# The second key's one-hot rows on ScalarE in three of four steps of the second gate half

## The chip, the core and the metric

The kernel runs on one NeuronCore of a Trainium2 chip. The time is device time in microseconds of one execution. TensorE multiplies matrices, VectorE and ScalarE work elementwise, GpSimd (POOL) issues the gathers, SyncE (SP) the large loads. A program decides on which engine each instruction stands and in which order; an engine takes its instructions in that order, and a semaphore holds it where data or a buffer is not ready.

## What is computed

Two layers of a hybrid backbone are applied to 128 context tokens and to 256 latent tokens. The part that matters here is PEER, a retrieval of single-neuron experts, at the end of each layer:

```python
s1 = einsum('thd,nd->thn', q[:, :, 0], k1)      # 8 heads, 128 first keys
s2 = einsum('thd,nd->thn', q[:, :, 1], k2)      # 128 second keys
v1, i1 = top_k(s1, 16);  v2, i2 = top_k(s2, 16)
...
top, pos = top_k(cand, 16)                      # 16 of the 256 sums per head
idx = i1 * 128 + i2 at pos;  g = softmax(top)
a = gelu(u_tab[idx] . x)
y = sum over head, k of g * a * v_tab[idx]
```

Each token chooses 8 x 16 = 128 of 16384 experts, and expert (i1, i2) has row 128 * i1 + i2 of the tables u and v.

## The kernel before

The 128 context tokens gather their rows from the tables (POOL, one gather of 128 rows at a time; VectorE multiplies them at L692 and L703). The 256 latent tokens do without a gather: all 16384 experts are computed densely, and a matrix of gates, zero for all but the chosen ones, masks the result. For block i of 128 experts (all second keys of first key i):

- **a_step** (L852) multiplies the u rows by the tokens and puts gelu of the result into the tile AR, two blocks at a time. In most of them the rows are split into a rounded part (uhi, by ScalarE, L846) and a rest (ulo, by VectorE, L847), so that three fast passes replace a slow one.
- **w_step** (from L857) makes the gates of 8 tokens for the 64 first keys of a half and multiplies them into AR. VectorE makes the one-hot rows m1 of the first key (L878) and e1 = m1 x gate (L883); e2 holds the one-hot rows of the second key, 8 tokens x 128 keys. Every second step VectorE makes e2 with one comparison (L876); in the others ScalarE makes it as relu(1 - |key - i2|), with one Abs for each token (L872) and one Relu over the tile (L874). TensorE multiplies e2 by e1, 16 matmuls of 64 columns (L890), into the PSUM tile psW, and VectorE multiplies psW into AR in two pieces (L897, the AR update).
- **o_step** (L926) multiplies two blocks of AR by the v rows and sums over all blocks in acc. In some of them AR is split into pp (L906 on ScalarE, L907 on VectorE) and v into vhi (L915) and vlo (L916).

AR holds 96 of the 128 blocks, so the work goes in two halves: the first 32 a_steps; the first gate half, 32 w_steps with 8 a_steps between; o_steps and a_steps in turn; the second gate half (hf = 1), 32 w_steps with 16 o_steps to go between; and the last 32 o_steps. This is done once in each layer. In layer 0 the second half also holds a modulation (matmuls psm) for layer 1.

```python
EA = 0.5
def frac(i, f):
    return int((i + 1) * f) > int(i * f)
```

`frac(n, EA)` says whether ScalarE makes the e2 of step n. e2, m1 and e1 come from a pool X with two buffers each, psW from a PSUM pool with two; so the e2 of a step can be written only when the matmuls of the step two before are done.

The order in which instructions stand on each engine isn't the order of the code: a scheduler reckons with durations of its own, and issues whichever piece of work it holds ready. It also decides where the o_step matmuls stand between the w_steps, and how the context's part and the latents' part of layer 1 interleave. A change of one instruction's engine can move rows everywhere behind it. In layer 1 the routing of the context ends in the tile ids (L676), the gathers need it, and each gather is multiplied on VectorE at L692; the latents' attention ends in out_proj (psol on TensorE, L524 and L525 on VectorE), a normalisation (L127 to L216), and m2xh (L147), from which the tokens for PEER are made.

Of the kernel before, what the change touches and what calls it, by code (L numbers as in the profile page):

```python
# [45 lines left out]
def tile_fn(ctx: ExitStack, tc, A, outs):  # L46
# [22 lines left out]
    def pS(tag, name):  # L69
        return banks[tag].tile([128, 512], F32, name=name, tag=tag)  # L70
# [679 lines left out]
    for l in range(DEPTH):  # L750
# [45 lines left out]
        with ExitStack() as es_:  # L796
# [15 lines left out]
            def AR(s, n):  # L812
                return ar[0][:, s:s + n, :] if s < 48 else ar[1 + (s >= 64)][:, (s - 48 if s < 64 else s - 64):(s - 48 if s < 64 else s - 64) + n, :]

            def seg_end(s):
                return 48 if s < 48 else 64 if s < 64 else NS
# [40 lines left out]
            def w_step(hf, n):  # L857
                t0 = n * TC
                rb = rt[t0 // 128]
                ts_ = slice(t0 % 128, t0 % 128 + TC)  # L860
                G = TC // TI
                e2 = X.tile([128, G, 128, TI], F16, name="e2", tag="e2")
                m1 = X.tile([128, G, HALF, TI], F16, name="m1", tag="m1")
                e1 = X.tile([128, G, 2, HALF, TI], F16, name="e1", tag="e1")

                def of_tokens(q):
                    return rb[:, q, ts_].rearrange("p (g t) -> p g t", t=TI)[:, :, None, :]

                if frac(n, EA):
                    nb_ = nid[t0 // 128]  # L870
                    for t in range(TC):
                        S.activation(e2[:, t // TI, :, t % TI], iota1, AF.Abs,  # L872
                                     bias=nb_[:, t0 % 128 + t:t0 % 128 + t + 1])
                    S.activation(e2, e2, AF.Relu, bias=1.0, scale=-1.0)  # L874
                else:
                    V.tensor_tensor(e2, iota16[:, None].to_broadcast([128, G, 128, TI]),  # L876
                                    of_tokens(1).to_broadcast([128, G, 128, TI]), op=OP.is_equal)
                mk_ = V.tensor_tensor(m1, iota16[:, None, hf * HALF:(hf + 1) * HALF].to_broadcast([128, G, HALF, TI]),  # L878
                                      of_tokens(0).to_broadcast([128, G, HALF, TI]), op=OP.is_equal)
                marks["W" if hf == 0 else "X"].append(mk_)  # L880
                g0 = t0 % 128 // TI
                gates = rg[t0 // 128][:, g0:g0 + G, :, None, :]
                V.tensor_tensor(e1, m1[:, :, None].to_broadcast([128, G, 2, HALF, TI]),  # L883
                                gates.to_broadcast([128, G, 2, HALF, TI]), op=OP.mult)
                pw = pS("t", "psW")
                pwv = pw.rearrange("p (t i) -> p t i", t=TC)
                for t in range(TC):
                    g, u = t // TI, t % TI
                    for q in range(2):
                        T.matmul(pwv[:, t, :], lhsT=e2[:, g, :, u], rhs=e1[:, g, q, :, u], start=(q == 0),  # L890
                                 stop=(q == 1))
                i = 0
                while i < HALF:
                    s0 = (hf * HALF + i) % NS
                    n_ = min(HALF - i, seg_end(s0) - s0)
                    av = AR(s0, n_)[:, :, t0:t0 + TC]
                    V.scalar_tensor_tensor(av, pwv[:, :, i:i + n_].rearrange("p t i -> p i t"), 1.0 / WSC, av, op0=OP.mult, op1=OP.mult)  # L897
                    i += n_
# [55 lines left out]
            for n in range(NW):  # L954
                w_step(0, n)
                if (n + 1) * PRE // NW > n * PRE // NW:
                    a_step(NA + n * PRE // NW)
# [3 lines left out]
            for n in range(NW):  # L961
                w_step(1, n)
                if (n + 1) * PRE // NW > n * PRE // NW:
                    o_step(NA - PRE + n * PRE // NW)
                if n % 8 == 7 and mods:
                    modulation(*mods.pop(0), "A")
# [30 lines left out]
            for k, r in RATES[l].items():  # L997
                ms = marks[k]
                n = int(len(ms) * r + 0.5)
# [14 lines left out]
EA = 0.5  # L1014
# [14 lines left out]
KA = 0.375  # L1029
KO = 0  # L1030
KO1 = 0


def frac(i, f):
    return int((i + 1) * f) > int(i * f)
# [6 lines left out]
def VSPLIT(l, ii):  # L1042
    return not frac(ii, KQ if NA - PRE <= ii < NA else KO if ii < 32 else KO1)

# [78 lines left out]
```

## Time and profile before

| | us |
|---|---|
| median of 3 runs (2414.77 to 2418.68) | 2416.36 |
| the profiled execution | 2407.9 |
| its span | 2406.1 |
| TensorE busy | 2260.6 |
| VectorE busy | 1904.6 |
| ScalarE busy | 1115.2 |
| second gate half, layer 0 | about 917 to 1045 |
| second gate half, layer 1 | about 2090 to 2214 |

The profiled execution is one of its own, 8.5 us shorter than the median of the runs; sums made from its rows are set against 2407.9. Busy time counts an engine's running instructions; matmuls overlap, so that TensorE counts as busy as long as they follow each other without a gap. The granted clock is the share of full speed at which TensorE was allowed to run in a stretch.

### The profile page before, as it was taken

Reading aid. Unit: us, or ns where it says so; the run is one execution under the profiler, and the core shown is the slowest. Engines: PE = TensorE matmul, PEld = TensorE weight load, DVE = VectorE, ACT = ScalarE, POOL = GpSimd, SP = SyncE. Lnnn points to the kernel's source line nnn. Section 1 sums busy time; section 2 is a strip of 40 time slices with the busy share of each in tenths; the row PEclk is TensorE's granted clock in tenths of the full one; section 3 lists DMA queues with packets and bytes.
Section 4 is the critical chain, followed back from the end, with each engine's and each line's share of the span. In section 5 each row is a group of like instructions: output and inputs, shape, how many; then the busy total and the mean of one; then the engine's idle time right before and its main releaser. Section 6 shows DMA issues by size and latency. Waiting matters only on the chain.

```text
span 2406.1 us, 41658 instructions
## 1 busy us (share of the span) xinstructions
PE 2260.6 (94%) x15660; PEld 1914.5 (80%) x15660; DVE 1904.6 (79%) x3942; ACT 1115.2 (46%) x2084; POOL 697.7 (29%) x523
## 2 busy tenths in 40 slices
PE   6999889999999999999989996989999999998997
PEld 5686469999998995667778785889999889855886
DVE  3157579996898888898863468899879888899987
ACT  3324532442785445444445553134348744444444
POOL 0000233454004433464200003435530143344630
PEclk8999989999999999999999998999999999998998
DMA  9967889999658999999863355989985599987994
GB/s 331 322 193 265 336 322 348 324 358 350 219 159 295 360 332 347 328 352 374 299 213 113 120 158 196 325 313 349 363 320 159 188 374 346 333 309 270 395 364 147
DMA packets 196314, 696.05 MB, mean 289 GB/s; under 512 B 22992, under 2 KB 27408, under 8 KB 196112
## 3 DMA queue, kind: packets, MB, share of 16 engines
q1 hardware_dynamic: 110016, 398.52, 46.7%
q0 software_dynamic: 74736, 272.14, 31.1%
q10 hardware_dynamic: 11360, 22.73, 2.8%
q8 instruction: 123, 2.02, 0.3%
q14 instruction: 79, 0.65, 0.1%
HBM read 689.14 MB, written 4.16 MB: 288 GB/s over the span
## 4 chain that ended last, share of the span: by engine, by line
PE 32%; DVE 8%; issue 8%; DMA 2%; POOL 1%; ACT 1%; DVEq 0%; ACTq 0%; POOLq 0%
PE acc L926 18%; PE psA L852 6%; DVE gt L692 2%; PE psil L262 2%; DMA gt<-in_peer_u_dram,ids 1%; POOL gt L686 1%; PE psqp L561 1%; PE psic L262 1%; DVE ulo L847 1%; PE psoc L522 1%; PE pssl L421 1%; DMA wic<-in_w_in_dram 1%; PE psW L890 0%; DVE idx L550 0%; DVE rep L548 0%
## 5 line engine op out<-in xcount | busy, mean ns | idle before, releaser
L686 POOL DMA_INDIRECT gt<-in_peer_u_dram,ids x256 | 325.3, 1271 | 1185.6 <-DVE gt L692 478.4
L686 POOL DMA_INDIRECT gt<-in_peer_v_dram,ids x256 | 368.0, 1438 | 464.0 <-DVE acc L703 434.7
L926 PE MATMUL acc<-vhi,pp 128*128 128x512 f32 x1728 | 441.9, 398 | 15.6 <-ACT pp L906 9.4
L852 PE MATMUL psA<-h2hi,uhi 128*128 128x256 f32 x1664 | 416.2, 287 | 5.1 <-ACT uhi L846 5.1
L852 PE MATMUL psA<-h2lo,uhi 128*128 128x256 f32 x1664 | 411.3, 284 | 0.0
L926 PEld LDWEIGHTS acc<-vhi,pp 128*128 128x128 f32 x1728 | 326.1, 191 | 86.3 <-ACT pp L906 10.0
L915 ACT ACTIVATE vhi<-v 128x1024 fp32r<-128x1024 f32 x216 | 228.7, 1060 | 274.0 <-PE acc L926 161.2
L692 DVE SCALAR_TENSOR_TENSOR gt<-gt,h2c 128x1024 f32<-128x1024 f32 x256 | 309.5, 1216 | 28.0 <-DMA gt<-in_peer_u_dram,ids 27.9
L703 DVE SCALAR_TENSOR_TENSOR acc<-gt,wcol,acc 128x1024 f32<-128x1024 f32 x254 | 325.5, 1282 | 6.2 <-DMA gt<-in_peer_v_dram,ids 5.2
L846 ACT ACTIVATE uhi<-u 128x1024 fp32r<-128x1024 f32 x208 | 220.0, 1058 | 230.2 <-PE psA L852 107.5
L852 PEld LDWEIGHTS psA<-h2hi,uhi 128*128 128x128 f32 x1664 | 319.7, 192 | 7.9 <-ACT uhi L846 5.7
L852 PEld LDWEIGHTS psA<-h2lo,uhi 128*128 128x128 f32 x1664 | 320.0, 192 | 2.1
L847 DVE TENSOR_TENSOR ulo<-u,uhi 128x1024 fp32r<-128x1024 f32 x208 | 254.3, 1223 | 79.9 <-ACT uhi L846 74.7
L916 DVE TENSOR_TENSOR vlo<-v,vhi 128x1024 fp32r<-128x1024 f32 x216 | 263.6, 1223 | 52.6 <-ACT vhi L915 47.7
L852 PE MATMUL psA<-h2hi,ulo 128*128 128x256 f32 x1664 | 239.4, 286 | 1.0 <-DVE ulo L847 0.8
L926 PE MATMUL acc<-vlo,pp 128*128 128x512 f32 x864 | 234.3, 392 | 1.5 <-DVE vlo L916 1.4
L852 PEld LDWEIGHTS psA<-h2hi,ulo 128*128 128x128 f32 x1664 | 216.2, 192 | 3.0 <-DVE ulo L847 1.6
L872 ACT ACTIVATE e<-iota,nid 128x128 f16<-128x128 f16 x512 | 158.9, 426 | 112.1 <-PE psW L890 112.1
L926 PEld LDWEIGHTS acc<-vlo,pp 128*128 128x128 f32 x864 | 162.3, 189 | 35.8 <-DVE vlo L916 2.5
L852 PE MATMUL psA<-h2T,u 128*128 128x256 f32 x768 | 171.8, 379 | 0.0
L852 PEld LDWEIGHTS psA<-h2T,u 128*128 128x128 f32 x768 | 143.1, 190 | 18.1
L926 PE MATMUL acc<-v,AR 128*128 128x512 f32 x320 | 143.6, 599 | 0.0
(437 smaller groups left out, 3039.9 us busy)
## 6 DMA issues: line engine op xcount, KB each, us to landing
u<-in_peer_uT_dram SPq DMA_DIRECT2D x256, 512.0 KB, 6.0
v<-in_peer_v_dram SPq DMA_DIRECT2D x256, 512.0 KB, 6.0
wm<-in_w_mod_dram SPq DMA_DIRECT2D x96, 512.0 KB, 7.2
wq<-in_peer_wq_dram SPq DMA_DIRECT2D x64, 512.0 KB, 4.7
wic<-in_w_in_dram SPq DMA_DIRECT2D x26, 512.0 KB, 5.7
wil<-in_w_in_dram SPq DMA_DIRECT2D x26, 512.0 KB, 4.2
woc<-in_w_o_dram SPq DMA_DIRECT2D x16, 512.0 KB
wol<-in_w_o_dram SPq DMA_DIRECT2D x16, 512.0 KB, 3.6
```

The source lines that it names most:

```text
L262: T.matmul(ps[:, :n], lhsT=ch.hT[b][:, c, :], rhs=wv[:, c, :], start=(c == 0), stop=(c == 7))
L421: T.matmul(sb[i][:, m * nk:(m + 1) * nk], lhsT=lhs(i, h), rhs=rhs(h), start=True, stop=True)
L686: nc.gpsimd.indirect_dma_start(out=t, out_offset=None, in_=tab, in_offset=bass.IndirectOffsetOnAxis(ap=pk.ids[:, j:j + 1], axis=0))
L692: V.scalar_tensor_tensor(t, t, 1.0, pk.h2c, op0=OP.mult, op1=OP.mult, accum_out=acol[:, j:j + 1])
L703: V.scalar_tensor_tensor(pk.acc, t, wcol[:, j:j + 1], pk.acc, op0=OP.mult, op1=OP.add)
L846: S.activation(hi, ua, AF.Copy)
L847: marks["A" if ii < NA else "U" if ii < NA + PRE else "B"].append(V.tensor_sub(lo, ua, hi.bitcast(F32)))
L852: T.matmul(ps[:, a * 256:(a + 1) * 256], lhsT=lw[:, c * 128:(c + 1) * 128], rhs=rw[:, c, :], start=(k == 0), stop=(k == len(passes) - 1))
L872: S.activation(e2[:, t // TI, :, t % TI], iota1, AF.Abs, bias=nb_[:, t0 % 128 + t:t0 % 128 + t + 1])
L915: S.activation(hi, v, AF.Copy)
L916: marks["O" if ii >= NA else "Q" if ii >= NA - PRE else "P"].append(V.tensor_sub(lo, v, hi.bitcast(F32)))
L926: T.matmul(accp[tb][h], lhsT=pl[:, tb * 128:(tb + 1) * 128], rhs=vr[:, h * 512:(h + 1) * 512], start=st0, stop=sp)
```

## The change

```diff
-                if frac(n, EA):
+                if frac(n, EA1 if hf else EA):
                     nb_ = nid[t0 // 128]
                     for t in range(TC):
                         S.activation(e2[:, t // TI, :, t % TI], iota1, AF.Abs,
                                      bias=nb_[:, t0 % 128 + t:t0 % 128 + t + 1])
                     S.activation(e2, e2, AF.Relu, bias=1.0, scale=-1.0)
                 else:
...
+EA1 = 0.75
```

In the second half, steps 1, 2, 3, 5, 6, 7 and so on are ScalarE's, steps 0, 4, 8 and so on VectorE's. Per layer 24 steps in place of 16 have an e2 from ScalarE. Nothing else is edited. The order moves with it, in two places that matter below.

**ScalarE, end of the second gate half of layer 1.** The rows from the last conversion of v for an o_step inside the half to the first pp behind it; each e2 with a number is one step, nid0 and nid1 hold the negated second keys of the two token blocks. Before:

```order
L872 ACTIVATE e2_21623<-iota1_234,nid1_14818 128x128 x8
L915 ACTIVATE vhi_21986<-v32_21984 128x1024
L874 ACTIVATE e2_21623<-e2_21623 128x1024
L872 ACTIVATE e2_21693<-iota1_234,nid1_14818 128x128 x8
L874 ACTIVATE e2_21693<-e2_21693 128x1024
L872 ACTIVATE e2_21763<-iota1_234,nid1_14818 128x128 x8
L874 ACTIVATE e2_21763<-e2_21763 128x1024
L872 ACTIVATE e2_21860<-iota1_234,nid1_14818 128x128 x8
L874 ACTIVATE e2_21860<-e2_21860 128x1024
L872 ACTIVATE e2_21930<-iota1_234,nid1_14818 128x128 x8
L874 ACTIVATE e2_21930<-e2_21930 128x1024
L906 ACTIVATE pp_21975<-AR2_17149 128x512
```

Now, the last six ScalarE steps (25, 26, 27, 29, 30, 31):

```order
L872 ACTIVATE e2_21805<-iota1_234,nid1_14882 128x128 x8
L872 ACTIVATE e2_21850<-iota1_234,nid1_14882 128x128 x6
L874 ACTIVATE e2_21805<-e2_21805 128x1024
L872 ACTIVATE e2_21850<-iota1_234,nid1_14882 128x128 x2
L874 ACTIVATE e2_21850<-e2_21850 128x1024
L872 ACTIVATE e2_21883<-iota1_234,nid1_14882 128x128 x8
L874 ACTIVATE e2_21883<-e2_21883 128x1024
L872 ACTIVATE e2_21980<-iota1_234,nid1_14882 128x128 x8
L872 ACTIVATE e2_22025<-iota1_234,nid1_14882 128x128 x8
L874 ACTIVATE e2_21980<-e2_21980 128x1024
L874 ACTIVATE e2_22025<-e2_22025 128x1024
L872 ACTIVATE e2_22058<-iota1_234,nid1_14882 128x128 x8
```

Before, Abs and Relu of a step follow each other, and every e2 is separated from the next by a step of VectorE. Now pairs and triples stand together, and Abs of the later step stand ahead of the Relu of the earlier. On TensorE, between the last o_step matmul inside the half and the first one behind it, there stood 128 matmuls of L890, eight steps; now there are 160, ten steps. In layer 0 there were 64, four steps, and are now 96, six steps.

**VectorE, layer 1, from the context's ids on** (psol is out_proj's result, y1 and y2 its sums for the two token blocks, gt a gathered block of rows). Before:

```order
L676 TENSOR_TENSOR ids_13834<-i1_13905,i2_13906 128x128
L524 TENSOR_TENSOR y1_14579<-psol_14705,g1_14577 128x128
L525 SCALAR_TENSOR_TENSOR y1_14579<-xl_11599,y1_14579 128x128
L524 TENSOR_TENSOR y1_14579<-psol_14718,g1_14577 128x128
L525 SCALAR_TENSOR_TENSOR y1_14579<-xl_11599,y1_14579 128x128
L127 BN_STATS la_st_14730<-y1_14579 128x6
L692 SCALAR_TENSOR_TENSOR gt_23280,acol_23278<-gt_23280,h2c_13451 128x1024
L128 BN_AGGR la_mv_14731<-la_st_14730 128x2
L524 TENSOR_TENSOR y2_14580<-psol_14743,g1_14577 128x128
L215 SCALAR_TENSOR_TENSOR y1_14579<-y1_14579,la_mv_14731,lnr0_14573 128x1024
L692 SCALAR_TENSOR_TENSOR gt_23283,acol_23278<-gt_23283,h2c_13451 128x1024
```

Now:

```order
L676 TENSOR_TENSOR ids_13898<-i1_13969,i2_13970 128x128
L525 SCALAR_TENSOR_TENSOR y2_14644<-xl_11663,y2_14644 128x128
L524 TENSOR_TENSOR y1_14643<-psol_14671,g1_14641 128x128
L525 SCALAR_TENSOR_TENSOR y1_14643<-xl_11663,y1_14643 128x128
L524 TENSOR_TENSOR y2_14644<-psol_14682,g1_14641 128x128
L525 SCALAR_TENSOR_TENSOR y2_14644<-xl_11663,y2_14644 128x128
L692 SCALAR_TENSOR_TENSOR gt_23408,acol_23406<-gt_23408,h2c_13515 128x1024
L524 TENSOR_TENSOR y1_14643<-psol_14695,g1_14641 128x128
L692 SCALAR_TENSOR_TENSOR gt_23411,acol_23406<-gt_23411,h2c_13515 128x1024
L525 SCALAR_TENSOR_TENSOR y1_14643<-xl_11663,y1_14643 128x128
L524 TENSOR_TENSOR y2_14644<-psol_14706,g1_14641 128x128
L692 SCALAR_TENSOR_TENSOR gt_23414,acol_23406<-gt_23414,h2c_13515 128x1024
```

The routing stands earlier against out_proj: six rows of L524 stood behind ids, now fourteen do, and rows of L692 stand between them. From ids to m2xh there were seven rows of L692, and now there are fifteen.

## Rows read from the trace of the kernel before

**Rows 1.** The page, first part: busy time (share of the span) and instructions.

```profile
PE 2260.6 (94%) x15660; PEld 1914.5 (80%) x15660; DVE 1904.6 (79%) x3942; ACT 1115.2 (46%) x2084; POOL 697.7 (29%) x523
```

**Rows 2.** Windows of both second halves: us, then busy us by engine, clock, DMA.

```profile
940.00:950.00 10.00, 5.04 (x98) 2.75 (x97) 10.00 (x19) 7.08 (x18) 2.42 (x2) 1.00 0.97 375
...
2180.00:2190.00 10.00, 10.00 (x57) 5.37 (x56) 9.63 (x14) 3.38 (x9) 4.70 (x3) 1.00 0.87 306
...
2200.00:2210.00 10.00, 4.13 (x64) 3.50 (x64) 10.00 (x20) 7.29 (x19) 1.87 (x2) 0.50 0.38 110
...
sum 150.00, PE 138.92 PEld 89.98 DVE 135.25 ACT 72.09 POOL 62.21; mean PE 9.26 PEld 6.00 DVE 9.02 ACT 4.81 POOL 4.15
```

**Rows 3.** Lines 872, 874, 876, one instruction: count, ns min/median/max, first and last start.

```profile
L872 ACT ACTIVATE e<-iota,nid x512: 417/425/451, 614.6 to 2208.9; 128x128 f16<-128x128 f16 x171
...
L874 ACT ACTIVATE e<-e x64: 1039/1054/1060, 617.9 to 2209.3; 128x1024 f16<-128x1024 f16 x64
...
L876 DVE TENSOR_TENSOR e<-iota,rt x64: 677/684/707, 612.0 to 2206.8; 128x1024 f16<-128x1024 f16 x64
```

**Rows 4.** Timeline of TensorE, layer 1, end of the half: start, us, line, [idle before].

```profile
2189.69 6.25 PE L926 MATMUL acc<-v,AR 128*128 128x512 f32 x14
2195.78 1.13 PE L890 MATMUL psW<-e,e 128*128 128x64 f16 x32
2198.47 0.65 PE L890 MATMUL psW<-e,e 128*128 128x64 f16 x16 [1.57 <-DVE e L883]
...
2205.67 1.03 PE L890 MATMUL psW<-e,e 128*128 128x64 f16 x16 [1.17 <-ACT e L874]
...
2213.78 3.78 PE L926 MATMUL acc<-vhi,pp 128*128 128x512 f32 x8 [1.75 <-ACT pp L906]
...
2222.13 1.98 PE L926 MATMUL acc<-vhi,pp 128*128 128x512 f32 x8
```

**Rows 5.** Timeline of ScalarE, same stretch, same columns.

```profile
2091.76 2.48 ACT L872 ACTIVATE e<-iota,nid 128x128 f16<-128x128 f16 x8 [1.97 <-PE psW L890]
2094.11 1.04 ACT L915 ACTIVATE vhi<-v 128x1024 fp32r<-128x1024 f32 x1
...
2189.95 2.49 ACT L872 ACTIVATE e<-iota,nid 128x128 f16<-128x128 f16 x8 [6.62 <-PE psW L890]
...
2202.04 2.48 ACT L872 ACTIVATE e<-iota,nid 128x128 f16<-128x128 f16 x8 [1.46 <-PE psW L890]
2204.56 1.06 ACT L874 ACTIVATE e<-e 128x1024 f16<-128x1024 f16 x1
```

**Rows 6.** Timeline of VectorE, same stretch, same columns.

```profile
2196.46 0.76 DVE L897 SCALAR_TENSOR_TENSOR AR<-psW,AR 128x256 f32<-128x256 f32 x2 [1.97 <-PE psW L890]
2197.13 0.68 DVE L876 TENSOR_TENSOR e<-iota,rt 128x1024 f16<-128x1024 f16 x1
2197.73 0.69 DVE L883 TENSOR_TENSOR e<-m,rg 128x1024 f16<-128x1024 f16 x1
...
2212.63 0.77 DVE L897 SCALAR_TENSOR_TENSOR AR<-psW,AR 128x256 f32<-128x256 f32 x2
```

**Rows 7.** Timeline of TensorE, layer 0, end of its second half.

```profile
1029.18 7.97 PE L926 MATMUL acc<-v,AR 128*128 128x512 f32 x18
1036.99 1.13 PE L890 MATMUL psW<-e,e 128*128 128x64 f16 x32
1041.84 0.84 PE L890 MATMUL psW<-e,e 128*128 128x64 f16 x16 [1.50 <-ACT e L874]
1045.00 3.78 PE L926 MATMUL acc<-vhi,pp 128*128 128x512 f32 x8 [2.31 <-ACT pp L906]
```

**Rows 8.** Waits of TensorE, 1045 to 1780 us (total, times, longest); page, fifth part.

```profile
PE m2pst L201 <- DVE m2xh L147: 11.1, 1, 11.1
...
L692 DVE SCALAR_TENSOR_TENSOR gt<-gt,h2c 128x1024 f32<-128x1024 f32 x256 | 309.5, 1216 | 28.0 <-DMA gt<-in_peer_u_dram,ids 27.9
```

## The prediction

> **What bounds the kernel now.** The first part of the page is read first: TensorE is busy for 94% of the span [rows 1]. Work moved between VectorE and ScalarE can therefore change the time only where TensorE is not fed. Next come the windows of the second gate half. In layer 1, from 2070 to 2220 us, TensorE is busy for 138.92 of 150 us, VectorE for 135.25 and ScalarE for 72.09 [rows 2]. The single windows show two regimes. At 2180 to 2190 TensorE is busy throughout: w_steps come in pairs, and between two pairs stand o_step matmuls which hide all that the other engines do. At 2200 to 2210 it is busy for 4.13 of 10 us, VectorE for 10.00, ScalarE for 7.29, and the granted clock is 0.50, the lower of its two levels [rows 2]. There the written order has used up the o_steps, and w_steps follow each other bare. I call this the tail.
>
> The timeline of TensorE gives the tail's size. In layer 1 the last covering matmuls end at 2189.69 + 6.25 = 2195.94, the next o_step starts at 2213.78 [rows 4]: 17.84 us for eight w_steps. In layer 0 it is 1029.18 + 7.97 = 1037.15 to 1045.00, so 7.85 us for four [rows 7]. The chain of a tail step now runs over VectorE: AR update, e2, e1, and only then the 16 matmuls (2196.46, 2197.13, 2197.73, then 2198.47) [rows 4, 6].
>
> **The operation that moves.** VectorE makes e2 in one instruction of 684 ns [rows 3]; its successor starts 0.60 after it [rows 6]. ScalarE needs eight Abs (425 ns each) and a Relu (1054 ns) [rows 3]; the Abs overlap, so the timeline is the price: Relu starts 2.52 after the first Abs and takes 1.06, together 3.58 us. Another instruction may start 2.35 after the first Abs (2091.76 to 2094.11) [rows 5]. Eight steps per layer move, 16 in all: VectorE loses 16 x 0.684 = 10.9 us, ScalarE gains 16 x 3.58 = 57.3.
>
> ScalarE thus pays 3.58 us for what costs VectorE 0.68 [rows 3, 5]. The Trainium skill, page "ScalarE: Activation LUTs", section "Rules for kernel authors", speaks against such a move: for relu, max, add and the like it advises VectorE, not ScalarE. By that rule every moved step is a loss, +46 us for sixteen by the rows' difference; the windows answer that an engine which idles for half of a stretch pays nothing there.
>
> **Covered pairs: nothing.** With 8 x 3.58 = 28.6 us more, ScalarE would be busy for about 101 of the 150 us in layer 1 [rows 2], still under TensorE. One detail decides whether that holds in each pair. e2 has two buffers, so ScalarE can start a pair only when the pair before has been multiplied. A pair with one ScalarE step needs 3.58 us; a new pair with two needs 2.35 + 2.52 + 1.06 + 1.06 = 7.0. An unsplit o_step matmul takes 0.443 us (7.97 us for 18) [rows 7]; in the new order the thinnest cover ahead of a double pair is 14 of them (6.2 us, before the tail of layer 0) and 16 (7.1 us, before that of layer 1), and ahead of the others there is more. So cover remains, thinly; if it is gone, a pair stalls by some 2 us (a rival below).
>
> **The tails.** The order shows what a count of busy time does not: because the scheduler reckons w_steps as slower, it lets more o_step matmuls pass ahead of them. In layer 1 ten w_steps are now left bare (22 to 31) instead of eight, in layer 0 six (26 to 31) instead of four. Two of four in a row were ScalarE's; now it is three, and only 24 and 28 are VectorE's. I walk layer 1 with t = 0 where the o_step matmuls end. Steps 22 and 23 were made under cover and run to 0.97, as the pair there does now (2195.78 + 1.13 - 2195.94) [rows 4]. Step 24 goes over VectorE as now, 2.5 to 3.1 (2198.47 - 2195.94 = 2.53, then 0.65). Step 25: ScalarE starts at 1.05 when 23 is done, but the order puts six Abs of step 26 ahead of the Relu, 14 Abs = 4.2 us, Relu to 6.4; matmuls 6.4 to 7.4 (1.03 each at the lower clock [rows 4]). Step 26: two Abs and Relu to 8.0, matmuls to 9.1. Step 27: 8.0 + 3.58 = 11.6, matmuls to 12.6; 28 follows to 13.6. Steps 29 and 30 need the buffers of 27 and 28: from 12.7, Relus end at 18.6 and 19.6, matmuls to 20.7. Step 31 needs 29's buffer, free at 19.7: e2 at 23.3, matmuls to 24.4. The last AR update, pp and the first o_step follow 1.15 after (2212.63 to 2213.78) [rows 4, 6]: 25.6 us. ScalarE is busy nearly throughout; VectorE, which had been the limit, now waits.
>
> The tail starts 0.97 earlier, since two steps fewer lie before it. Layer 1: 25.6 - 17.84 - 0.97 = **+6.8 us**. In layer 0 steps 26 to 31 repeat the pattern of 22 to 27: last matmuls 11.6 to 12.6, o_step at 13.8. 13.8 - 7.85 - 0.97 = **+5.0 us**. Lowest for the two: if the Abs of two steps cost no extra latency (25 and 26 two us earlier in each), +8 together; highest: no two e2 overlap, and after step 24 (at 3.1) each ScalarE step takes 3.58 + 1.03, six and three of them: 31.9 and 18.1 us with the 1.15, +22 together. I take the walk, +11.8, since the rows show Abs of one set running into the next instruction. The restart at the low clock (eight matmuls in 3.78 us against 1.98 later [rows 4]) is paid in both kernels: no term.
>
> **Other places.** In layer 0, at 940 to 950, TensorE is idle for 5 us while w_steps meet modulation matmuls and VectorE is at 10.00 [rows 2]. The new order has one w_step fewer in this group, but with ScalarE chains in it: between -5 and +5, taken as 0. The first gate half keeps its engines: 0. The front of layer 1 is re-ordered though nothing there was edited. The routing of the context comes earlier, which can save up to the 11.1 us that TensorE waits for m2xh [rows 8]; fifteen instead of seven products with gathered rows (L692, 1.216 us [rows 8]) now stand between ids and m2xh, 8 x 1.22 = 9.8 us at worst, more if a gather is late, since everything behind it on VectorE waits. The two nearly cancel: -11 to +10, taken as -1. POOL and SP issue the same DMAs in the same numbers.
>
> **Sum:** 6.8 + 5.0 + 0 + 0 - 1 = +10.8, say **+11 us**. Against the profiled execution, 2407.9 us, that is 2418.9; the median of the runs, 2416.36, lies 8.5 us above that execution, so the forecast is 2416.36 + 11 = **2427.4 us**. About 0.2% (4.8 us) is what a measurement of this kernel can tell from no change.
>
> **Rivals.**
> 1. The tails as walked: 62%, 2427.4, own range 2418 to 2436.
> 2. Faster, by VectorE's relief. Where VectorE is full and TensorE idle (940 to 950, and the wait for m2xh), 10.9 us of relief and the earlier routing shorten the stretch. It decides if the front of layer 1 gains more than the two tails lose, that is if the 11.1 us wait goes altogether and the bad pattern of the tails costs only its lower bound: 8 - 11 - 4 (of the five idle us) = -7, 2409 us. For it speaks that VectorE is at 10 of 10 just there; against it the eight extra products. 10%.
> 3. Nothing measurable: the tails cost 8 to 12 and the front gives about as much back, 2416. 13%.
> 4. Slower still: the pairs stall too. The conversions of v (L915, 1.04 us [rows 5]) queue behind an e2 that waits for its buffer; 7.0 us plus two conversions is 9.1, more than the shortest covers. Four double pairs per layer with 1 to 2 us each make 8 to 12 more: about 2437. Against it: ScalarE now sits idle for 6.62 us ahead of an e2 near the end [rows 5]. 12%.
> 5. The full difference of the two rows, 16 x (3.58 - 0.68) = +46 us, 2462: it would need ScalarE to be the limit in all of the stretch, against 72.09 busy of 150 [rows 2]. 3%. The rule of the Trainium skill, page and section as above, points this way.
>
> That the change does not do what it says is excluded by the order: 24 of 32 e2 are ScalarE's.
>
> **Range and chances.** Rival 1's own range, extended to rival 3 below and to the upper bound of the tails and most of rival 4 above: 2415 to 2438; left out are rivals 2 and 5 and the edge of 4, under 2 in 10. Slower by over 0.2%: 62 + 12 + 3 = 77%; within: 13%; faster: 10%.
>
> **What would show it.** In the changed profile the last covering o_step of layer 1 is followed by ten w_steps and about 25 us without o_step matmuls, of layer 0 by six and about 14; in these TensorE waits for ScalarE's Relu (L874) and no longer for VectorE's e1. Between pairs TensorE stays at 10 of 10. L876 falls from 64 to 48 instructions. I am wrong if the tails stay near 18 and 8 us, if TensorE stalls between pairs, or if the time between 1240 and 1560 changes by more than the tails do.

## The result and the profile after

The change makes the kernel slower: a median of 2444.22 us against 2414.34 for before on the same chip, six runs each; the ratio is 1.0138, 95% interval 1.0120 to 1.0156, some 33 us. The forecast was 2427.4, its range ended at 2438. The profiled execution of the changed kernel took 2438.4 us with a span of 2436.6, that of before 2407.9 and 2406.1; the 30.5 us between the spans are what follows.

The page's first part (busy time, share of the span, instructions) answers to [rows 1]:

```profile
PE 2271.0 (93%) x15660; PEld 1920.1 (79%) x15660; DVE 1894.1 (78%) x3922; ACT 1171.4 (48%) x2236; POOL 669.8 (27%) x523
```

TensorE's share has fallen from 94 to 93%, though the same 15660 matmuls keep it busy for 10.4 us more. Of the 30.5 us, 20.1 are idle time of TensorE and 10.4 longer busy time, at a mean granted clock of 0.963 instead of 0.972. Where they lie, the timeline of TensorE shows. First the tail of layer 0 (start, duration, instruction, and in brackets the idle time before it and what ended it), for [rows 7]:

```profile
1035.03 6.25 PE L926 MATMUL acc<-v,AR 128*128 128x512 f32 x14
1041.12 1.13 PE L890 MATMUL psW<-e,e 128*128 128x64 f16 x32
1044.10 0.65 PE L890 MATMUL psW<-e,e 128*128 128x64 f16 x16 [1.85 <-DVE e L883]
1047.65 1.04 PE L890 MATMUL psW<-e,e 128*128 128x64 f16 x16 [2.90 <-ACT e L874]
1049.36 1.03 PE L890 MATMUL psW<-e,e 128*128 128x64 f16 x16 [0.67 <-ACT e L874]
1052.82 1.03 PE L890 MATMUL psW<-e,e 128*128 128x64 f16 x16 [2.43 <-ACT e L874]
1055.04 3.78 PE L926 MATMUL acc<-vhi,pp 128*128 128x512 f32 x8 [1.18 <-ACT pp L906]
```

The covering matmuls end at 1041.28, the next o_step starts at 1055.04: 13.76 us where it was 7.85. The tail of layer 1, for [rows 4]:

```profile
2211.58 7.11 PE L926 MATMUL acc<-v,AR 128*128 128x512 f32 x16
2218.52 1.13 PE L890 MATMUL psW<-e,e 128*128 128x64 f16 x32
2221.22 0.66 PE L890 MATMUL psW<-e,e 128*128 128x64 f16 x16 [1.57 <-DVE e L883]
2225.23 1.04 PE L890 MATMUL psW<-e,e 128*128 128x64 f16 x16 [3.35 <-ACT e L874]
2226.94 1.04 PE L890 MATMUL psW<-e,e 128*128 128x64 f16 x16 [0.68 <-ACT e L874]
2230.39 1.89 PE L890 MATMUL psW<-e,e 128*128 128x64 f16 x32 [2.42 <-ACT e L874]
2237.31 1.98 PE L890 MATMUL psW<-e,e 128*128 128x64 f16 x32 [5.03 <-ACT e L874]
2242.07 1.03 PE L890 MATMUL psW<-e,e 128*128 128x64 f16 x16 [2.78 <-ACT e L874]
2244.29 3.78 PE L926 MATMUL acc<-vhi,pp 128*128 128x512 f32 x8 [1.18 <-ACT pp L906]
```

From 2218.69 to 2244.29 it is 25.60 us where it was 17.84. TensorE's waits ahead of L890 (us in all, times) have turned round. Before:

```profile
  DVE e L883: 12.1, 8
  ACT e L874: 6.1, 5
```

After:

```profile
  ACT e L874: 24.8, 11
  DVE e L883: 3.4, 2
```

VectorE's e1 was the releaser; now it is ScalarE's Relu. VectorE is no less busy for it. The window over the new tail of layer 1 (columns as further below) has it at 24.98 of 25.60 us, where it was at 17.32 of 17.84:

```profile
2218.69:2244.29 25.60, 8.60 (x161) 7.50 (x157) 24.98 (x45) 21.16 (x56) 8.44 (x7) 0.58 0.51 156
```

The sums over gathered rows (L703, 1.28 us each) fill it, nine of them where there were five. But the two tails have grown by 5.9 and 7.8 us, less than half of the 30.5. The rest lies where nothing was edited. I call **front of layer 1** the stretch from the last o_step matmul of layer 0 (in what follows, the mark) to the last matmul of the latents' query scores (L566). One window over it (start and end, length, busy us of TensorE, its weight loads, VectorE, ScalarE and GpSimd with instructions, granted clock, DMA share, GB/s), before and after:

```profile
1238.01:1579.62 341.61, 303.79 (x2027) 257.78 (x2026) 225.74 (x799) 145.87 (x400) 49.50 (x46) 0.96 0.56 187
```

```profile
1249.10:1609.93 360.83, 308.18 (x1998) 258.54 (x1997) 235.51 (x828) 149.86 (x405) 56.51 (x55) 0.92 0.57 191
```

360.8 us instead of 341.6. TensorE runs 29 matmuls fewer in it, idles 52.7 us instead of 37.8, and is busy 4.4 us longer, at a mean granted clock of 0.92 instead of 0.96. The account of the spans, all from marks of the two timelines: up to layer 0's tail +4.1 (of which +3.8 stands there at the first gate matmul, 619.3 against 623.1 us, with the same order up to it), tail of layer 0 +5.9, from there to the end of layer 0's o_steps +1.1, front +19.2, from the front to the tail of layer 1 -7.6, that tail +7.8, behind it 0: 30.5.

### The profile page after: what moved, and what is told of

It reads as the page before. It is cut to its first block, busy times and chain, and to the rows that moved or that the text cites. A ratio compares the mean times of both kernels' runs of the same rounds, so it can differ in the third digit from the quotient of the medians.

```text
span 2436.6 us, 41824 instructions
## 1 busy us (share of the span) xinstructions
PE 2271.0 (93%) x15660; PEld 1920.1 (79%) x15660; DVE 1894.1 (78%) x3922; ACT 1171.4 (48%) x2236; POOL 669.8 (27%) x523
## 4 chain that ended last, share of the span: by engine, by line
PE 76%; DVE 10%; DMA 7%; ACT 4%; issue 2%; POOL 1%; ACTq 0%; DVEq 0%; SPq 0%; POOLq 0%
PE acc L926 30%; PE psA L852 27%; PE psil L262 3%; DVE gt L692 3%; DMA gt<-in_peer_u_dram,ids 3%; PE psqp L561 3%; PE psW L890 2%; DMA wm<-in_w_mod_dram 2%; PE psic L262 2%; PE pssl L421 1%; PE psm L166 1%; DMA wic<-in_w_in_dram 1%; PE psoc L522 1%; PE psol L522 1%; ACT e L872 1%
## 5 line engine op out<-in xcount | busy, mean ns | idle before, releaser
L686 POOL DMA_INDIRECT gt<-in_peer_u_dram,ids x256 | 317.6, 1241 | 1222.8 <-DVE gt L692 495.5
L686 POOL DMA_INDIRECT gt<-in_peer_v_dram,ids x256 | 347.8, 1359 | 484.7 <-DVE acc L703 443.8
L926 PE MATMUL acc<-vhi,pp 128*128 128x512 f32 x1728 | 442.1, 398 | 14.8 <-ACT pp L906 11.3
L692 DVE SCALAR_TENSOR_TENSOR gt<-gt,h2c 128x1024 f32<-128x1024 f32 x256 | 309.0, 1214 | 35.8 <-DMA gt<-in_peer_u_dram,ids 34.8
L703 DVE SCALAR_TENSOR_TENSOR acc<-gt,wcol,acc 128x1024 f32<-128x1024 f32 x254 | 324.5, 1277 | 9.6 <-DMA gt<-in_peer_v_dram,ids 8.9
L872 ACT ACTIVATE e<-iota,nid 128x128 f16<-128x128 f16 x640 | 196.7, 426 | 91.9 <-PE psW L890 82.9
```

What stands on the lines that cost most here:

```text
L686: nc.gpsimd.indirect_dma_start(out=t, out_offset=None, in_=tab, in_offset=bass.IndirectOffsetOnAxis(ap=pk.ids[:, j:j + 1], axis=0))
L692: V.scalar_tensor_tensor(t, t, 1.0, pk.h2c, op0=OP.mult, op1=OP.mult, accum_out=acol[:, j:j + 1])
L703: V.scalar_tensor_tensor(pk.acc, t, wcol[:, j:j + 1], pk.acc, op0=OP.mult, op1=OP.add)
L872: S.activation(e2[:, t // TI, :, t % TI], iota1, AF.Abs, bias=nb_[:, t0 % 128 + t:t0 % 128 + t + 1])
L926: T.matmul(accp[tb][h], lhsT=pl[:, tb * 128:(tb + 1) * 128], rhs=vr[:, h * 512:(h + 1) * 512], start=st0, stop=sp)
```

## What happened in the front

The scheduler lays the program along its own reckoning of the engines' times. Steps moved in layer 0's gate half alone change how it lays layer 1 (l0only below); why they do is not shown. In the changed kernel it puts the context's output projection (L522, psoc) ahead of the latents' attention (scores: L421, pssl), where before it was spread between their scores. From the last latents' projections (L262, psil) on, TensorE's timeline of before:

```profile
1339.10 1.92 PE L262 MATMUL psil<-wil,hT 128*128 128x32 f32 x8
1340.95 1.65 PE L421 MATMUL pssl<-kTl,qTl 64*128 64x384 f32 x2
1342.52 4.33 PE L522 MATMUL psoc<-woc,mTc 128*128 128x128 f32 x22
...
1368.86 2.05 PE L522 MATMUL psoc<-woc,mTc 128*128 128x128 f32 x16
```

and after:

```profile
1348.15 2.62 PE L522 MATMUL psoc<-woc,mTc 128*128 128x128 f32 x22
1350.61 3.07 PE L262 MATMUL psil<-wil,hT 128*128 128x128 f32 x26
...
1364.43 0.31 PE L262 MATMUL psil<-wil,hT 128*128 128x32 f32 x2
1364.67 0.91 PE L421 MATMUL pssl<-kTl,qTl 64*128 64x384 f32 x2
...
1369.05 2.05 PE L522 MATMUL psoc<-woc,mTc 128*128 128x128 f32 x16
```

Before, the latents' projections end at 1341.02, which is 103.0 us after the last o_step of layer 0 (the mark, 1238.01), their scores start at once, and the context's output projection fills TensorE between them until 29.9 us later. Now 96 of its 128 matmuls (12.2 us) stand ahead of the last latents' projections, where 10 (1.5 us) did. The projections end 115.6 us after the mark (1249.10), and 6.4 us later the output projection is used up: the scores come late and have little beside them (TensorE waits 4.9 us for their softmax, 0.8 before, and from 1380 to 1400 us the granted clock is 0.75). They end 222.8 us after the mark instead of 207.9, the latents' output projection 264.0 instead of 246.6. The latents are the chain that is waited for: their normalised rows (m2xh) are what TensorE stands still for next. Along this chain the delay is 12.6 us at the end of the projections, 14.9 at the end of the scores, 17.4 at the end of the output projection and 18.8 at m2xh; two thirds of it are there before the piece of VectorE that comes next begins.

On VectorE the context's ids come as early as before (235.2 us after the mark, 235.3 before), but the latents' sums are late. The ids and m2xh before:

```profile
1473.30 0.29 DVE L676 TENSOR_TENSOR ids<-i,i 128x128 int32<-128x128 f32 x1
...
1494.79 0.81 DVE L147 TENSOR_SCALAR m2xh<-xl,m_mv,m_rs 128x1024 f32<-128x1024 f32 x1
```

and after:

```profile
1484.25 0.28 DVE L676 TENSOR_TENSOR ids<-i,i 128x128 int32<-128x128 f32 x1
...
1524.71 0.81 DVE L147 TENSOR_SCALAR m2xh<-xl,m_mv,m_rs 128x1024 f32<-128x1024 f32 x1
```

So between the first product with gathered rows (L692) and m2xh there now stands this (groups of instructions: count, busy us, mean ns, idle us before them). Before, in 16.7 us:

```profile
L692 DVE SCALAR_TENSOR_TENSOR gt<-gt,h2c 128x1024 f32<-128x1024 f32 x7 | 8.5, 1214 | 2.5 <-DMA gt<-in_peer_u_dram,ids 2.5
...
L524 DVE TENSOR_TENSOR y<-psol,g 128x128 f32<-128x128 f32 x4 | 1.1, 272 | 0.0
L525 DVE SCALAR_TENSOR_TENSOR y<-xl,y 128x128 f32<-128x128 f32 x4 | 1.0, 283 | 0.0
```

After, in 34.8 us:

```profile
L692 DVE SCALAR_TENSOR_TENSOR gt<-gt,h2c 128x1024 f32<-128x1024 f32 x15 | 18.2, 1213 | 4.8 <-DMA gt<-in_peer_u_dram,ids 4.7
L525 DVE SCALAR_TENSOR_TENSOR y<-xl,y 128x128 f32<-128x128 f32 x12 | 3.4, 284 | 0.1
L524 DVE TENSOR_TENSOR y<-psol,g 128x128 f32<-128x128 f32 x12 | 3.4, 282 | 0.3 <-PE psol L522 0.3
```

Fifteen products instead of seven (18.2 us, not 8.5), twelve pairs of sums instead of four (6.8 us, not 2.1), and 4.7 us of waiting for gathers instead of 2.5. These three make 16.6 of the 18.1 us by which this piece is longer, and m2xh comes 18.8 us later. They say what fills the piece; whether the latents could have come sooner without them, they do not say. TensorE's waits (for [rows 8]):

```profile
PE m2pst L201 <- DVE m2xh L147: 12.5, 1, 12.5
...
PE psT L436 <- ACT pt L430: 6.0, 1, 6.0
...
PE m2pst L201 <- ACT m2xh L149: 3.9, 1, 3.9
```

The wait for m2xh on VectorE, 11.1 us in [rows 8], has not gone; it is 12.5. The wait for the second m2xh, which ScalarE makes (L149), was 7.1 us and is 3.9, so some 3 us are won back there. The 6.0 us for pt (L430) are new. They lie at 1276 to 1283, where TensorE reaches the transposes of the first context heads with only 12 projection matmuls ahead of them; ScalarE is then on the softmax, and the order has put one reciprocal root of a layer norm (L137) in the middle of four exponentials (L426). ScalarE's timeline:

```profile
1276.24 1.28 ACT L426 ACT_TABLE_LOAD   x1
...
1278.70 1.28 ACT L137 ACT_TABLE_LOAD   x1
1280.00 0.20 ACT L137 ACTIVATE m_q<-m_q 128x1 f32<-128x1 f32 x1
1280.22 1.28 ACT L426 ACT_TABLE_LOAD   x1
```

Two table loads of 1.28 us for one instruction of 0.20.

## Experiments

Theory 1: the tails cost what the prediction said, and the other 20 us are the order of the front. Theory 2: the price follows the number of steps that ScalarE takes over, 30 us for 16, wherever they stand. Theory 3: layer 1's tail sets everything behind it back. All kernels below differ from the changed one in the condition of the one edited line, but for two, where it is said. Each was compared with runs of before on the same chip.

**One layer at a time, and single steps**

Only layer 1 (l1only):

```diff
-                if frac(n, EA1 if hf else EA):
+                if frac(n, EA1 if hf and l else EA):
```

> Only layer 1 has three of four steps on ScalarE; TensorE's order from layer 0 to the first gate step of layer 1 is that of before, word for word. Theory 1 (the 20 us that the prediction lacks are the new order of the front of layer 1, which the scheduler lays differently): only layer 1's longer tail is left, +8 us against before (5 to 11), and the front lasts as long as before. Theory 2 (each step that ScalarE takes over costs its share wherever it is, 30 us over 16 steps): +15 us. Theory 3 (layer 1's tail sets all behind it back): +25 to +30 us.

Ratio 1.0022 (1.0007 to 1.0037), +5.3 us. Front 339.0 us, tail of layer 1 25.59. That is all that the longer tail costs by itself, and theory 3 falls.

Only layer 0 (l0only):

```diff
+                if frac(n, EA1 if hf and not l else EA):
```

> Only layer 0 has three of four steps on ScalarE; the front of layer 1 has the order of the changed kernel, word for word, the tail of layer 1 its eight bare steps of before. Theory 1 (order of the front): +6 for layer 0's tail, about +20 in the front, some 6 of it given back behind: +18 to +25 us. Theory 2 (by the number of steps): +15 us. Theory 3 (layer 1's tail): +5 us.

Ratio 1.0078 (1.0058 to 1.0097), +19 us. Front 362.3, tails 13.66 and 18.08. Layer 0 has as many moved steps as layer 1 and costs over three times as much; theory 2 falls. The two layers together make 24 us, 9 less than the change. The intervals still meet (the two reach up to 9 and 23 us, the change's goes down to 29), but no run explains the gap.

One covered step of layer 0 (s14):

```diff
+                if frac(n, EA1 if hf and not l and n == 14 else EA):
```

> One step more on ScalarE, step 14 of layer 0's second half, under cover; front of layer 1 and both tails in the order of before. Theory 1 (order): within 3 us of before. Theory 2 (by the number of steps): +2 us. If it stands more than 5 us off, a covered step does cost something, and the term that I set to nothing is wrong.

Ratio 0.9999 (0.9987 to 1.0012), front 338.0. A covered step costs nothing that shows; but the interval is 3 us to either side, about what one step would cost by the two rows (3.58 - 0.68 = 2.9). The kernel l1p20 below, with five covered steps, is the stronger test.

Steps 26 and 30 of each layer (tail24):

```diff
+                if frac(n, EA1 if hf and n >= 24 else EA):
```

> Three of four steps on ScalarE from step 24 on alone, so steps 26 and 30 of each layer move and no other; the tails keep 4 and 8 bare steps as before, the front of layer 1 has the order of the changed kernel, word for word. Theory 1 (order of the front): about +20 in the front, some 6 given back, 0 to 4 for each tail: +14 to +22 us with a quarter of the change's moved steps. Theory 2 (by the number of steps): +7.5 us. The prediction's tails alone: 0 to +8 us.

Ratio 1.0102 (1.0082 to 1.0122), +24.6 us, with a quarter of the moved steps; 14 to 22 were expected by theory 1, and the lower end of the interval (20) lies within that. The window over its front:

```profile
1248.05:1605.86 357.81, 307.56 (x1998) 259.24 (x1997) 235.39 (x828) 150.07 (x405) 55.32 (x55) 0.92 0.57 192
```

That is 357.8 us, with the changed kernel's 1998 matmuls. The tails, at the old four and eight bare steps, took 13.08 and 21.73: more ScalarE rows lengthen a tail by themselves, by 5.2 and 3.9.

**A third order**

Step 30 of layer 0 alone (s30):

```diff
+                if frac(n, EA1 if hf and not l and n == 30 else EA):
```

> One step more on ScalarE than before, step 30 of layer 0's second half. The scheduler answers with a third order of layer 1's front, neither that of before nor that of the changed kernel; both tails keep 4 and 8 bare steps. Theory 1 (the order sets the front's time): the front lasts something other than the 338 to 342 us of before's order, of either sign, and the kernel stands off before by that difference plus 0 to 4 us in layer 0's tail. Theory 2 (by the number of steps): +2 us with a front of 338 to 342 us.

Ratio 1.0008 (0.9993 to 1.0023), front 343.9, tail of layer 0 9.46. With +1.9 us in all this run alone decides nothing between the theories; it is the partner of the next.

Steps 0 to 23 of both layers (pre24):

```diff
+                if frac(n, EA1 if hf and n < 24 else EA):
```

> Three of four steps on ScalarE in steps 0 to 23 of both layers, every second behind: 12 of the change's 16 moved steps. The tails hold 6 and 10 bare steps as in the changed kernel, the front of layer 1 has the third order, that of the kernel with step 30 alone, word for word. Theory 1 (order): the front lasts as long as in that kernel, within 3 us, and the whole is 8 to 14 us longer than it (two tails of 6 and 7, less what step 30 costs its tail). Theory 2 (by the number of steps): 11 steps at 1.9 us, 21 us longer than the kernel with step 30 alone, +23 us against before.

Ratio 1.0056 (1.0036 to 1.0076), +10 us to the kernel with step 30 alone by the medians. Its front is

```profile
1243.78:1589.30 345.52, 307.39 (x2061) 264.47 (x2061) 228.62 (x824) 149.82 (x406) 46.18 (x46) 0.94 0.57 192
```

345.5 us, within 1.6 of its sister's; the tails 12.85 and 22.84. Twelve of sixteen moved steps cost little over half of what four cost above.

**Is it the tables?** The kernel with steps 26 and 30, with another first estimate of one reciprocal root in layer 1 (t24est). LAY[0] holds the number of the layer; the lines that set it are left out here:

```diff
-        S.activation(y, ve, AF.Abs_reciprocal_sqrt)
+        V.tensor_scalar(y, ve, -0.5, 1.5, op0=OP.mult, op1=OP.add) if name == 'm1' and LAY[0] else S.activation(y, ve, AF.Abs_reciprocal_sqrt)
```

> As the kernel with steps 26 and 30 moved, but in layer 1 the first estimate of the reciprocal root in the layer norm of the second latent block is 1.5 - 0.5 v on VectorE instead of a table function on ScalarE. TensorE's order is that kernel's, word for word; on ScalarE the two table loads of 1.28 us between the four exponentials of the first context heads are gone. If this switch of tables makes the 6.0 us wait of the transposes and the low clock behind it, the wait falls to about 3 us and the front from 358 to between 348 and 353 us. If the wait only moves (the front is bound elsewhere, as by the context routing), the front stays at 355 to 359 us.

TensorE's wait fell as expected:

```profile
PE psT L436 <- ACT pt L430: 3.1, 1, 3.1
```

but the front did not follow:

```profile
1246.51:1606.41 359.90, 306.21 (x1998) 257.73 (x1997) 235.53 (x829) 146.52 (x402) 56.84 (x55) 0.93 0.57 191
```

359.9 us, ratio 1.0094 (1.0074 to 1.0114). Of the two cases expected, the one in which the tables set the front (348 to 353 us) did not come; it is the other, a front bound elsewhere, 0.9 us above its 355 to 359. Against the kernel without the new estimate (tail24), the latents' projections end 2.4 us earlier after the mark, ids 2.1 earlier, and m2xh 0.2 later. The gain is lost on VectorE, which waits for the gathers in the piece before m2xh, here

```profile
DVE gt L692 <- DMA gt<-in_peer_u_dram,ids: 6.9, 5, 2.2
```

and in tail24

```profile
DVE gt L692 <- DMA gt<-in_peer_u_dram,ids: 4.6, 5, 2.3
```

So the 6.0 us at the first heads are visible but do not bind here: in this order m2xh is held by VectorE, with the products ahead of it and their gathers.

**VectorE in the tail.** The kernel before, its steps unchanged, with fewer gathers hung on the second gate half of layer 1 (bg20):

```diff
-                marks["W" if hf == 0 else "X"].append(mk_)
+                (hf == 0 or l == 0 or n < 20) and marks["W" if hf == 0 else "X"].append(mk_)
```

> The kernel before, with its steps as they were; in layer 1 the marks of the second gate half on which context gathers are hung end with step 19, so that the gathers' accumulations go behind the tail: 2 instead of 5 of 1.29 us stand between VectorE's last twenty gate multiplications. Front of layer 1 in the order of before, word for word. If VectorE binds the bare steps of layer 1's tail (17.3 of 17.84 us busy), the tail shortens by 2 to 4 us and the kernel is 1 to 4 us faster than before. If ScalarE's rows bind it, the tail stays at 17 to 18 us and the time within 2 us. If the gathers that are pushed back come late for the last layer norm, it is 2 to 6 us slower.

Ratio 1.0002 (0.9989 to 1.0016). The tail is 16.69 us, 1.15 less, with one such product in it where before's has five: four of 1.29 us taken away gave back a fifth of their time. A miss in the size, 2 to 4 us were expected. VectorE is busy for only 12.95 us of this tail (17.32 before), ScalarE for 11.29, and it is nearly as long as before, so neither engine's busy time alone sets it. That the chain from engine to engine does is likely, but not shown.

**The same rows, other orders**

The change with one of its sixteen steps undone (m2):

```diff
+                if frac(n, EA1 if hf and (l or n != 2) else EA):
```

> The changed kernel with one of its sixteen moved steps undone: step 2 of layer 0's second half, far from the tail, goes back to VectorE. Both tails keep their 6 and 10 bare steps, but the scheduler now lays the front of layer 1 nearly as before: the context's output projection ends behind the latents' projections again. Theory 1 (order): the front falls from 358 to 362 us back to 338 to 346, and the kernel is +9 to +17 us against before, some 15 to 20 less than the changed one. Theory 2 (by the number of steps): 15/16 of the change, +28 to +31 us.

Ratio 1.0056 (1.0037 to 1.0074), +13.5 us. Its front:

```profile
1252.33:1591.91 339.58, 301.78 (x2029) 256.96 (x2028) 225.93 (x799) 145.70 (x400) 51.62 (x46) 0.96 0.57 189
```

339.6 us; the tails are 15.14 and 25.58. One covered step put back, the first of the eight moved ones of layer 0, returns some 20 of the 33 us.

The whole number of rows, with another remainder left to VectorE in layer 0, 2 (p2) or 3 (p3):

```diff
+                if (n % 4 != 2) if hf and not l else frac(n, EA1 if hf else EA):
```

> All rows of the change, 24 of 32 steps on ScalarE in both layers, but in layer 0 VectorE keeps the steps whose number leaves 2 when divided by 4 instead of 0. Both tails have 6 and 10 bare steps; in the front of layer 1 the context's output projection ends behind the latents' projections, as before. Theory 1 (order): front of 338 to 346 us, tails of 12 to 15 and 22 to 26, +9 to +18 us against before. Theory 2 (by the number of steps): +30 us.

```diff
+                if (n % 4 != 3) if hf and not l else frac(n, EA1 if hf else EA):
```

> As the kernel that keeps remainder 2 on VectorE, but with remainder 3: the same number of rows on each engine, the same bare steps in the tails, and a front of layer 1 almost as in the changed kernel, with the context's output projection ahead of the latents' attention. Theory 1 (order): front of 356 to 363 us, +26 to +36 us against before, some 15 to 20 more than its sister. Theory 2 (by the number of steps): the same time as its sister.

Ratios 1.0054 (1.0035 to 1.0074) and 1.0138 (1.0113 to 1.0163), that is +13 and +33 us. The fronts, remainder 2 and then remainder 3:

```profile
1251.83:1593.13 341.30, 303.33 (x2030) 259.89 (x2029) 225.35 (x804) 146.55 (x400) 45.39 (x44) 0.94 0.56 185
```

```profile
1256.17:1616.97 360.80, 302.19 (x1998) 255.31 (x1997) 235.01 (x826) 149.33 (x403) 56.85 (x55) 0.94 0.57 191
```

341.3 and 360.8 us, with tails of 16.00 and 25.58, and 17.72 and 25.58 (12 to 15 were expected for layer 0). Two kernels with the same rows on the same engines are 20 us apart, and their fronts 19.5.

**Only the early steps of layer 1** (l1p20):

```diff
+                if frac(n, EA1 if hf and l and n < 20 else EA):
```

> Only steps 2, 6, 10, 14 and 18 of layer 1 move; from step 20 on every second step is ScalarE's, as before. The front of layer 1 has the order of before, word for word, but the scheduler leaves ten bare steps in layer 1's tail instead of eight. If the longer tail comes from the two more bare steps alone, at before's 2.2 us each, the tail is 21 to 23 us and the kernel +2 to +5 us; if it comes from ScalarE's rows in the tail (25.6 us with them), the tail stays at 18 us and the time within 2 us. If VectorE's relief under cover is worth something, it is faster than before by 2 us or more.

Ratio 1.0007 (0.9992 to 1.0023), +1.7 us, tail 22.84 us. Ten bare steps at the old mix cost 5.0 us more than eight, as tail24 showed 3.9 for the mix alone. Five covered steps moved; by the rows that would be 14.5 us, and TensorE waits nowhere between the last split psA and the tail. Relief of VectorE under cover brought nothing that shows.

The marks of all of them in one table (us, from each one's profiled execution):

| kernel | tail, layer 0 | front, layer 1 | tail, layer 1 | ratio to before |
|---|---|---|---|---|
| before | 7.85 | 341.6 | 17.84 | |
| changed | 13.76 | 360.8 | 25.60 | 1.0138 |
| l1only | 8.48 | 339.0 | 25.59 | 1.0022 |
| l0only | 13.66 | 362.3 | 18.08 | 1.0078 |
| s14 | 9.53 | 338.0 | 17.84 | 0.9999 |
| tail24 | 13.08 | 357.8 | 21.73 | 1.0102 |
| s30 | 9.46 | 343.9 | 17.84 | 1.0008 |
| pre24 | 12.85 | 345.5 | 22.84 | 1.0056 |
| t24est | 13.43 | 359.9 | 21.73 | 1.0094 |
| bg20 | 8.39 | 339.4 | 16.69 | 1.0002 |
| m2 | 15.14 | 339.6 | 25.58 | 1.0056 |
| p2 | 16.00 | 341.3 | 25.58 | 1.0054 |
| p3 | 17.72 | 360.8 | 25.58 | 1.0138 |
| l1p20 | 7.84 | 339.5 | 22.84 | 1.0007 |

The fronts fall in two groups, 338 to 346 and 358 to 362, and the order goes with them: the context's output projection ends 29 to 31 us after the latents' projections in the short ones, 6 to 8 after them in the long ones. A second property goes with them as well: between ids and m2xh stand fifteen products with gathered rows in all the long ones, one to seven in the short ones. No run has one of the two without the other. No version beat the kernel before.

## Why the prediction was wrong

**What bounds, and the price of a row: right.** In the second gate halves TensorE waits only in bare stretches and among the modulation matmuls; covered steps cost nothing that shows (s14, l1p20).

**The tails: right, in layer 1 nearly to the digit.** The walk gave layer 1 matmuls of step 24 at 2.5, of 25 at 6.4, of 27 at 11.6, of 31 at 23.3 to 24.4 and the o_step at 25.6 us; measured from 2218.69 they start at 2.53, 6.54, 11.70 and 23.38, and the o_step at 25.60. Layer 0: 13.8 against 13.76, but that digit is partly luck, for with six bare steps of the same mix the tail is 13.66 in l0only and 15.14 in m2, and with four steps as before it is 7.84 to 9.53. The 0.97 for two steps fewer ahead of the tail holds in layer 1: from the last split psA to the tail it was 113.2 us, now 112.2. Layer 1 alone cost +5.3 (1.7 to 8.9) as a whole kernel, forecast 6.8. The walk did not separate two causes that the runs did: two more bare steps (+5.0) and more ScalarE rows (+3.9) each lengthen it, and together give 7.8. One sentence of it is wrong, "VectorE, which had been the limit, now waits": VectorE is busy for 24.98 of the 25.60 us, filled up with sums over gathered rows, and bg20 shows that its busy time alone was not the limit.

**Modulation stretch and first gate half: right at 0.** From the first gate matmul to layer 0's tail it was 417.8 us and is 418.2, so the 0.97 counted for layer 0 does not show. Counted from cover to cover, seven w_steps stand among the modulation matmuls instead of six, and that stretch takes 14.8 us instead of 13.9. In the modulation stretch TensorE still waits ahead of gate matmuls, 4.6 us for ScalarE's Relu now; between covered pairs, nowhere.

**The step that failed** is the one on the front of layer 1: "The two nearly cancel: -11 to +10, taken as -1." It measured +19.2, outside its own bounds. Both halves were wrong. The gain rested on "the routing of the context comes earlier", which was read from the order; in time the ids stand at 235.2 us after the mark as at 235.3 before, so nothing of the 11.1 us wait went. The loss, eight more products at 9.8 us, was there at 9.7 us, but it was not the worst case: the latents' own chain was already 12.6 us late at the end of its projections, eight more pairs of sums (4.7 us) stood behind ids as well, and the gathers held VectorE up for 2.2 more. The listing of VectorE had the pairs of sums (fourteen rows of L524 instead of six), and the sum gave them no term. What I left out was the order of TensorE ahead of it: the output projection of the context had moved ahead of the latents' projections (96 of its matmuls instead of 10), and I followed VectorE's rows only.

**Left out altogether:** some of the loss is given back. From the front's end to the last split psA it is 503.1 us before and 496.5 after, and 494.7 to 498.5 in the four other kernels with the late front, while seven of the others with an early one lie at 504 to 507 (m2 at 513.9). VectorE is busy 235.5 instead of 225.7 us in the long front: the products with gathered rows done there need not be done later. That this is the reason was not tried.

**The rivals.** Rival 4 came nearest in time, 2437, for a reason that did not occur. Rival 2's mechanism, the front deciding more than the tails, was the right place with the wrong sign. Rival 5's full row bill is refuted by l1only (8 x 2.9 = 23 us by the rows, 5.3 measured) and l1p20. The Trainium skill's advice behind it (page "ScalarE: Activation LUTs", section "Rules for kernel authors": such element-wise work to VectorE) is not borne out under cover (0.9999 in s14) and is in the tails (3.9 to 5.2 us more in tail24). The text's own test, that I am wrong "if the time between 1240 and 1560 changes by more than the tails do", is what came true.

**What stays open:** whether the late latents' chain or the products ahead of m2xh would alone make the front long. p2 has one product there instead of seven, and its m2xh comes 3.7 us earlier after the mark than before's, but its front gains nothing by it (341.3 us); t24est has an earlier chain and gains nothing either; a kernel with one and not the other was not made. Nor was it tried what in the scheduler's state tips the order.

## What to carry to other kernels

Where a scheduler lays out the whole program, an edit has two prices: what it does to the work around it, and what it does to the order of all that follows. The first can be walked from rows, and gave the tails to a tenth of a microsecond here, in layer 0 partly by luck; the second has no natural size. Here the front changed by up to 21 us between kernels that differ in one to sixteen steps (and lies at 338.0 to 341.6 us in the five kernels that have it in the order of before), so a prediction should give it a range of that width, and compare on every engine in which order two chains share it, the chain that is waited for above all. A tuned number that looks bad should be tried in a neighbouring version with the same work (another remainder, one step less) before the idea is dropped: here the idea costs 13 us and the order 20.

## What was not expected of the hardware

One ScalarE instruction of 0.20 us between exponentials brought two table loads of 1.28 us each. Taking all three away (t24est against tail24) shortened a wait on TensorE by 2.9 us (6.0 to 3.1), close to their 2.76, without moving the end: VectorE then waited for gathers 6.9 us instead of 4.6. The Trainium skill, page "ScalarE: Activation LUTs", section "What ACT_TABLE_LOAD costs", gives 1283 ns for a load, which the rows repeat, and 2.66 us for a switch with its drain. By that figure two switches would be worth an estimated 5.3 us. The rows above show no such drain: the load follows the last instruction, and the next follows the load, within 0.02 us. The absolute time of a mark is worth little across executions: the tail of layer 0 begins at 1037.15 us in before, 1046.82 in s14 and 1051.20 in bg20. Of the 9.7 and 14.1 us by which it is later there, 8.2 and 13.4 stand already at the first gate matmul, ahead of every edited row. Distances between marks repeat better: the front in the order of before is 338.0 to 341.6 us in five kernels.
